# The first layer's output product: seven products over 1024 of its 1536 rows, or over all of them

## The chip, the core and the metric

The kernel runs on one NeuronCore of one Trainium2 chip. TensorE (PE) multiplies; VectorE (DVE) and ScalarE (ACT) do the elementwise work and empty PE's accumulators in PSUM; GpSimd (POOL) does small arithmetic and issues the transfers that add to their target on arrival; SyncE (SP) issues the other transfers. The metric is the device time of one execution in microseconds. An execution that was profiled has its own time and, inside it, the span of the trace.

## The reference

Two encoder layers over 512 tokens of width 1024. Layer 0 mixes by dilated window attention (8 heads, three dilations each), layer 1 by grouped attention; both also attend with 4 heads to 256 memory tokens. What matters here is the end of each layer, with its 1536 = 8 x 128 + 4 x 128 branch columns:

```python
    for i in range(DEPTH):
        h = rmsnorm(x, norm_g[i])
        mem_h = rmsnorm(mem, mem_norm_g[i])
        ...
        o_mem = memory_attention(q_mem, mem_h, w_mem_kv[i], mem_qn_g[i], mem_kn_g[i])
        y = jnp.concatenate([o_mix, o_mem], axis=-1) * jax.nn.silu(gate)
        x = x + jnp.einsum('bse,ed->bsd', y, w_out[i])
```

y is [512 tokens, 1536], w_out[i] is [1536, 1024]. In this document the 1536 rows of w_out[0] are named by the heads that feed them: the memory heads 8 to 11 (m), heads 0 to 3 (a) and heads 4 to 7 (b), 512 rows each.

## The kernel before

**Float32 in three passes.** Each weight tile of 128x1024 ("wl", half a megabyte) is loaded, cast by ACT to PE's rounded format ("wh", L324), and DVE takes the rest ("wo" = wl - wh, L334). The activations have a high and a low half too. A product is then high x high (L177), low x high (L178) and high x low (L181): L177 and L178 are issued together and need wh alone, L181 follows at the end of a group and needs wo.

**Seven products instead of eight.** `s_chunk` multiplies 2x2 block matrices with seven block products (12, 11, S1, S2, S4, S3, 22, in this order), from sums of weight tiles (T1 to T4) and of activation tiles (S1 to S4). Each product of 512x512 blocks is summed over the rows in groups. A **group** is 12 matmuls of 128x512 (or 24 of 128x256 for the gates and projections) that use up one weight tile; PE's work is a row of groups, and I call each a **slot**. The two halves of 128 tokens of a block go to two PSUM banks ("pj", four in all, handed out in turn; four more, "at", serve attention). A product marked True in `PRODUCTS` starts with cleared banks taken anew ("fresh"), one marked False adds to what its bank holds.

**The order is fixed when the program is built.** `Driver` steps a set of generators once a slot (`tick`); what they issue goes to the engines' queues in that order, and each engine works through its own queue strictly in order, waiting on semaphores. `drv.late` puts an instruction at the end of a slot's list, `drv.soon` at the beginning of the next one's, `drv.release(gen, d)` starts the emptying of a bank d slots on. `W` plans the weights by `PLAN`: loads on SP ("wl<-in_wall"), sums by DVE, or by transfers that POOL issues (L262, L298, L308), wh on ACT, wo on DVE, about two slots ahead of their use.

**The end of layer 0.** The eight heads and the three gates follow `A_ORDER`: heads 0 to 7, then the gates m, a, b. A gate (seven products of 128x256 matmuls) yields SiLU values (ACT L883, DVE L885), which are multiplied by the heads' outputs, reloaded from DRAM ("og", L861, L870; the product is DVE L875, L879). For m and a the results ("yf") are turned into the activations y12, y11, yS1, ... of the output product by `prep_y` (ACT L924 high half, DVE L925 low half; sums L940 to L955). Head 7's last part (`attn_a`: scales on ACT L1414, transposes on PE L1430, values on PE L1451) runs during the output product, with pauses from `Y`.

`out_proj` runs the output product in two pieces. Heads 8 to 11 and 0 to 3 (1024 rows) go through `s_chunk` in seven products of two groups, 14 slots. Each product's bank is copied by ACT to "acc" (L400) or added to it by DVE (L423), and the residual x is added to acc by a transfer (L1012). Then `out_rest` takes heads 4 to 7 (512 rows) as a plain product: 8 groups, each emptied by a DVE add into acc (L815). When both halves of a row block are done, `ev_o` stores x1, norms it (ACT squares L526, POOL L487, DVE L533) and transposes it into the inputs of layer 1 (PE L539). The memory keys and values of layer 1 (8 slots) are multiplied between this and the first product of layer 1, and cover that chain.

Counting slots from the start of the program, the gates take slots 141 to 161, the seven products 162 to 175, the plain product 178 to 185 (176 and 177 hold no PE work), the memory product 186 to 193, and layer 1 starts at 194. In the trace slot 162 starts at 561.1 us, slot 178 at 603.9, slot 186 at 627.4 and slot 194 at 652.8.

## Time and profile before

| what | value |
|---|---|
| median of three runs | 938.81 us (938.36 to 940.7) |
| profiled execution, its own time | 938.24 us |
| span of its trace | 936.5 us |
| busy in the span: PE, DVE, ACT, POOL | 928.6, 798.3, 691.4, 347.4 us |
| granted TensorE clock, mean | 1.000 |
| HBM read, written | 160.41 MB, 13.17 MB |

Most of the working below compares the profiled execution with itself, so 938.24 us is the scale of its sums; it lies 0.57 us under the median. In the profile's rows, "out<-in" names tiles, "x4" counts instructions, and a group's "idle before" tells what ended the engine's idle time. A matmul's listed duration is a latency; matmuls overlap, so what one costs is the distance between the starts of two. In the chain of waits, a piece is start, length, engine, tile, line.

### The profile page before, as it was taken

What the parts mean: (1) busy time and instruction counts of PE and PEld (TensorE: products, weight loads), DVE (VectorE), ACT (ScalarE), POOL (GpSimd) and SP (SyncE); (2) the same over time, 40 slices, a digit from 0 to 9 for tenths busy, and PEclk for the clock granted to TensorE, in tenths of its full rate; (3) what the DMA queues carried; (4) which work ended last, traced back from release to release, by engine and by line L of the source; (5) the groups of instructions that cost most, each with busy time, mean ns of one, the idle gap of its engine ahead of it and who ended that gap; (6) DMA issues with size and microseconds to landing.
All of it is one profiled execution on the core that took longest, in us unless ns stands there. A gap on an engine that the chain in (4) does not pass through costs nothing.

```text
span 936.5 us, 16241 instructions
## 1 busy us (share of the span) xinstructions
PE 928.6 (99%) x5468; PEld 816.2 (87%) x5468; DVE 798.3 (85%) x1442; ACT 691.4 (74%) x1720; POOL 347.4 (37%) x496
## 2 busy tenths in 40 slices
PE   8999999999999999999999999999999999999998
PEld 6889888888888888888889998888988999999886
DVE  6998677879888888879798999977998998789977
ACT  6775789677868686867675768547878887789774
POOL 3411425556554545463836111214162440111122
PEclk9999999999999999999999999999999999999999
DMA  9999948968687778686867989979995686785777
GB/s 345 387 266 332 296 129 211 322 150 241 166 243 174 237 162 266 158 270 135 269 154 210 249 232 218 300 245 313 273 199 114 175 243 166 197 215 131 197 164 180
DMA packets 83789, 209.25 MB, mean 223 GB/s; under 512 B 18937, under 2 KB 28665, under 8 KB 83706
## 3 DMA queue, kind: packets, MB, share of 16 engines
q1 hardware_dynamic: 63178, 142.74, 42.7%
q0 software_dynamic: 19520, 63.97, 37.0%
q10 hardware_dynamic: 1008, 1.51, 0.4%
q8 instruction: 43, 0.70, 0.3%
q14 instruction: 40, 0.33, 0.1%
HBM read 160.41 MB, written 13.17 MB: 185 GB/s over the span
## 4 chain that ended last, share of the span: by engine, by line
PE 95%; DVE 2%; ACT 1%; DMA 1%; issue 0%; SPq 0%; DVEq 0%; ACTq 0%
PE pj L177 25%; PE pj L178 25%; PE pj L181 25%; PE qT L654 3%; PE sa L1342 2%; PE oo L1451 2%; PE ptb L1657 1%; PE sa L1338 1%; PE xT L539 1%; PE pt L1430 1%; PE ob L181 1%; PE ob L178 1%; PE ob L177 1%; PE sb L172 1%; PE sb L171 1%; PE sb L173 1%
## 5 line engine op out<-in xcount | busy, mean ns | idle before, releaser
L334 DVE TENSOR_TENSOR wo<-wl,wh 128x1024 fp32r<-128x1024 f32 x258 | 316.4, 1232 | 7.0 <-ACT wh L324 6.8
L324 ACT CAST wh<-wl 128x1024 fp32r<-128x1024 f32 x258 | 271.9, 1060 | 31.3 <-PE pj L178 18.7
L177 PE MATMUL pj<-wh,hS 128*128 128x512 f32 (+1 forms) x416 | 154.4, 380 | 0.0
L178 PE MATMUL pj<-wh,hS 128*128 128x512 f32 (+1 forms) x416 | 149.0, 367 | 0.0
L177 PE MATMUL pj<-wh,h 128*128 128x512 f32 (+1 forms) x312 | 115.2, 378 | 0.0
L178 PE MATMUL pj<-wh,h 128*128 128x512 f32 (+1 forms) x312 | 111.6, 367 | 0.0
L487 POOL TENSOR_TENSOR rstd<-mse,half 128x4 f32<-128x4 f32 (+2 forms) x98 | 104.1, 1062 | 8.2
L181 PE MATMUL pj<-wo,hS 128*128 128x512 f32 (+1 forms) x416 | 99.5, 366 | 0.0
L178 PEld LDWEIGHTS pj<-wh,hS 128*128 128x128 f32 x416 | 78.7, 189 | 11.3
L177 PEld LDWEIGHTS pj<-wh,hS 128*128 128x128 f32 x416 | 78.6, 189 | 11.1 <-DVE sn L423 0.2
L486 POOL TENSOR_SCALAR mse<-hss 128x4 f32<-128x4 f32 (+1 forms) x88 | 47.1, 535 | 101.3 <-ACT junk L642 93.5
L181 PEld LDWEIGHTS pj<-wo,hS 128*128 128x128 f32 x416 | 72.5, 189 | 13.2
L642 ACT ACTIVATE junk<-sn 128x128 f32<-128x128 f32 x264 | 79.3, 310 | 2.2 <-DVE sn L413 2.1
L400 ACT COPY sn<-pj 128x512 f32<-128x512 f32 x122 | 67.3, 590 | 17.7 <-PE pj L181 17.7
L1285 POOL TENSOR_TENSOR ta<-sn,tabs 128x128 f32<-128x128 f32 (+1 forms) x64 | 35.8, 566 | 117.5 <-DVE sn L647 90.4
L181 PE MATMUL pj<-wo,h 128*128 128x512 f32 (+1 forms) x312 | 74.5, 365 | 0.0
L308 POOL DMA_DIRECT2D wl<-wl x34 | 30.2, 897 | 111.4 <-DVE wo L334 71.9
L262 POOL DMA_DIRECT2D wl<-in_wall_dram x40 | 38.0, 966 | 80.8 <-DMA wl<-in_wall_dram 32.2
L423 DVE TENSOR_TENSOR sn<-pj,sn 128x512 f32<-128x512 f32 x89 | 60.8, 684 | 6.9 <-PE pj L181 6.6
L178 PEld LDWEIGHTS pj<-wh,h 128*128 128x128 f32 x312 | 59.0, 189 | 8.3
L177 PEld LDWEIGHTS pj<-wh,h 128*128 128x128 f32 x312 | 59.0, 189 | 8.2
L181 PEld LDWEIGHTS pj<-wo,h 128*128 128x128 f32 x312 | 54.3, 189 | 9.7
(284 smaller groups left out, 2358.5 us busy)
## 6 DMA issues: line engine op xcount, KB each, us to landing
wl<-in_wall_dram SPq DMA_DIRECT2D x224, 512.0 KB, 9.2
wl<-wl POOLq DMA_DIRECT2D x68, 512.0 KB, 5.6
wl<-in_wall_dram POOLq DMA_DIRECT2D x44, 512.0 KB, 8.4
od<-o SPq DMA_DIRECT2D x11, 256.0 KB, 3.6
og<-od SPq DMA_DIRECT2D x10, 256.0 KB, 8.6
x<-in_x_dram SPq DMA_DIRECT2D x4, 512.0 KB, 9.1
v0r<-sn SPq DMA_DIRECT2D x8, 256.0 KB, 10.9
v0d<-v0r SPq DMA_DIRECT2D x4, 512.0 KB
```

Of the source, the lines that this page charges most:

```text
L177: T.matmul(o, a, b, start=start, stop=False, skip_group_check=True)
L178: T.matmul(o, c, d, start=False, stop=False, skip_group_check=True)
L181: T.matmul(o, a, b, start=False, stop=stop, skip_group_check=True)
L262: queue.dma_start(t, wall[d], **how)
L324: A.copy(wh, self.tile[self.items[i]])
L334: V.tensor_tensor(wo, self.tile[key], wh.bitcast(F32), ALU.subtract)
L400: A.copy(t_, b_)
L423: V.tensor_tensor(t_, b_, t_, ALU.subtract if q == "12" else ALU.add)
L486: G.tensor_scalar(e, ss, EPS, None, ALU.add)
L487: G.tensor_tensor(r, e, half[:, 0:n], ALU.pow)
L642: A.activation(jk, p[:, j * 128:(j + 1) * 128], AF.Square, scale=by, accum_out=ss[:, j:j + 1])
L1285: G.tensor_tensor(ta[:, 0:n], xn[:, 0:n, 0:32], ropeA[:, 0, b, s0:s0 + n], ALU.mult)
```

## The change

Heads 4 to 7's rows are no longer a separate plain product. A new weight kind, `W3`, loads 12 blocks of two tiles' width for **one** set of seven products over all 1536 rows: each product has three groups, two for the rows of m and a, and a third for the rows of b (heads 4 to 7), which takes its activations from a second set, `YL` (tiles "yl11", "ylS1" and so on), made by `prep_l`: high half by ACT L994, low half by DVE L997, sums by DVE (L1020 makes the one for ylS1). The products come in the order 11, S3, 12, S1, S2, S4, 22. `out_rest` and its additions go. The gates are computed in the order b, m, a. The evacuations are new: `hold` copies 11, S3 and S1's banks; `add_11` copies and adds by a transfer; `fold` sums by transfers and one DVE subtraction; x is added by transfers from `ahead` (for 22 and 21) and `ev_all` (for 11 and 12). T1's weight sums are made by a transfer from layer 0's last chunk on (`T1_DMA` 15). Head 7 takes its pauses from `Y_LAST`. `ev_o` is stepped when both halves are done, whichever is last.

```diff
-Y = [3, 2, 2, 2, 3, 2, 2, 1, 1, 1]
-
-A_ORDER = "01234567mab"
-
-PLAN = ["W2"] + ["T2"] * 2 + ["W1", "W2s"] + ["W2" if c.isdigit() else "W1" for c in A_ORDER[1:]] + ["W2"] + ["O1"] * 2 + ["T2b"] * 2 + ["W1bs", "W2c"] + ["W1b"] * 4 + ["W2b", "W1o"]
+Y, Y_LAST = [3, 2, 2, 2, 3, 2, 2, 1, 1, 1], [2, 2, 1, 1, 2, 1, 1, 1, 1, 1]
+
+A_ORDER = "01234567bma"
+
+PLAN = ["W2"] + ["T2"] * 2 + ["W1", "W2s"] + ["W2" if c.isdigit() else "W1" for c in A_ORDER[1:]] + ["W3"] + ["T2b"] * 2 + ["W1bs", "W2c"] + ["W1b"] * 4 + ["W2b", "W1o"]
 SEQ = [1, 2, 0] + list(range(3, len(PLAN)))
 T4_AT = {4: 4}
-T1_DMA = 17
+T1_DMA = 15
...
+    ORDER_3 = ("11", "T3", "21", "T1", "T2", "22", "T4")
+    LOADS_3 = (("11", "11"), ("T3", "12"), ("21", "21"), ("T1", "12"), ("T2", "22"), ("22", "22"))
...
-                    for k in ORDER:
+                    order, loads = ORDER, LOADS
+                    if kind == "W3":
+                        order, loads, n = ORDER_3, LOADS_3, 3
+                        for k in at:
+                            at[k].append(d + 8 + 2 * (k[1] == "2") + (k[0] == "2"))
+                    self.allocs += [((c, k, x), at[q][x], kind) for k, q in loads for x in range(n)]
+                    for k in order:
                         for x in range(n):
...
+    PRODUCTS_3 = (("11", 1, True), ("S3", 0, True), ("12", 0, True), ("S1", 0, True), ("S2", 1, False), ("S4", 0, False), ("22", 0, True))
+
...
+        def hold(name, u, b):
+            t = snap[name, u] = place({"z": "11", "s3": "21", "s5": "22"}[name], u)
+            A.copy(t, b)
+            yield 1
+            if name == "s5":
+                ahead("22", u, t)
+
+        def add_11(name, u, b):
+            t = s2(name="sn")
+            A.copy(t, b)
+            yield 1
+            G.dma_start(snap[name, u], t, accum_op=ALU.add)
+            yield 1
+            yield from ev("11", u, snap[name, u])
+
+        def fold(name, u, b):
+            t, t3, t5 = place("12", u), snap["s3", u], snap["s5", u]
+            snap[name, u] = t
+            A.copy(t, b)
+            yield 1
+            G.dma_start(t3, t, accum_op=ALU.add)
+            yield 2
+            V.tensor_tensor(t5, t5, t3, ALU.subtract)
+            ahead("21", u, t3)
+            yield 1
+            yield from ev("22", u, t5)
+
         after = ((keep, "z"), (add, "11", "z"), (keep, "s5"), (keep, "s2"), (add, "12", "s2"), (keep, "s3"), (add, "21", "s3"))
-        for i, (a, s, fresh) in enumerate(PRODUCTS[:6] + (("22", 1, False),) if tail else PRODUCTS):
+        order, runs = PRODUCTS[:6] + (("22", 1, False),) if tail else PRODUCTS, K // per
+        if late is not None:
+            order, runs = PRODUCTS_3, 3
+            after = (hold, "z"), (hold, "s3"), (add_11, "z"), (hold, "s5"), (fold, "s2"), (add, "12", "s2"), (add, "21", "s3")
+        for i, (a, s, fresh) in enumerate(order):
             while a not in act:
                 drv.tick()
             if fresh:
                 bank[s] = [pj() for _ in range(units)]
-            for x in range(K // per):
+            for x in range(runs):
+                far = late is not None and x == 2
+                while far and a not in late:
+                    drv.tick()
                 wh, wo = [...]
+                ah, al = [(late if far else act)[a][:, v] for v in range(2)]
...
+                        d = 2 if f in (keep, hold, fold) or late is not None or tight and i == 1 else 2 + u + (units == 1 and i == 6 and not soon)
...
-    def out_rest(ys, acc, done, evac):
...
+            if fused:
+                yield from wait((0, 0))
+                put("11", a11)
+                yield 1
+                yield from wait((0, 1))
+                s1 = [s2(name="ys") for _ in range(2)]
+                for j in range(2):
+                    V.tensor_tensor(s1[j], a11[j], a21[j], ALU.subtract)
+                yield 1
+                put("S3", s1)
+                yield 1
...
+                put("12", a12)
...
+                    V.tensor_tensor(a21[j], a21[j], a22[j], ALU.subtract)
+                yield 1
+                put("S1", a21)
...
+            if fused:
+                while ys[0] is None:
+                    yield 1
+                put("11", ys[0])
+                yield 1
+                while ys[1] is None:
+                    yield 1
+                s1 = s2(name="yl")
+                V.tensor_tensor(s1, ys[0], ys[1], ALU.subtract)
+                put("S3", s1)
+                yield 1
+                while ys[2] is None:
+                    yield 1
+                put("12", ys[2])
+                yield 1
+                while ys[3] is None:
+                    yield 1
+                a11, a21, a12, a22 = ys
+                V.tensor_tensor(a21, a21, a22, ALU.subtract)
+                put("S1", a21)
+                yield 2
+                V.tensor_tensor(a11, a21, a11, ALU.subtract)
+                put("S2", a11)
...
+        def ev_all(q, u, t):
+            b, n = 2 * (int(q[0]) - 1) + u, int(q[1]) - 1
+            if not b // 2:
+                G.dma_start(t, src[b][:, n * 512:(n + 1) * 512], accum_op=ALU.add)
+                yield 2
+            done.add((n, b))
+            if {(0, b), (1, b)} <= done:
+                yield from evac(n, b, acc[b])
+
+        def ahead(q, u, t):
+            b, n = 2 + u, int(q[1]) - 1
+            G.dma_start(t, src[b][:, n * 512:(n + 1) * 512], accum_op=ALU.add)
+
+        if not last:
+            s_chunk(512, YW, ev_all, half=half, tight=True, place=place, late=YL, ahead=ahead)
+            return
+        drv.spawn(prep_l())
         s_chunk(512, YW, ev, half=half, tight=True, place=place)
-        if not last:
-            out_rest(ys, acc, done, evac)
-            return
...
-        yield Y[7] + (h == 7)
+        yield Y[7]
...
-            if c == "b":
+            if c == A_ORDER[-1]:
                 drv.spawn(prep_y(), PREP_Y)
+                drv.spawn(ys[0](), PREP_Y)
...
-        if n:
-            for j in range(2):
-                nc.sync.dma_start(x1d[b][:, j * 512:(j + 1) * 512], x1[j])
-            r = norm_1(x1)
-            yield EO[0]
-            norm_2(x1, r, rows["x1"])
-            yield EO[1]
-            if b < 2:
-                first_t(H2, x1, b)
-            else:
-                yield from diffs_t(H2, x1, b - 2)
-                yield EO[2]
-                yield from rest_t(H2, b - 2, (EO[3] + b - 2, *EO[4:]), True)
+        for j in range(2):
+            nc.sync.dma_start(x1d[b][:, j * 512:(j + 1) * 512], x1[j])
+        r = norm_1(x1)
+        yield EO[0]
+        norm_2(x1, r, rows["x1"])
+        yield EO[1]
+        if b < 2:
+            first_t(H2, x1, b)
+        else:
+            yield from diffs_t(H2, x1, b - 2)
+            yield EO[2]
+            yield from rest_t(H2, b - 2, (EO[3] + b - 2, *EO[4:]), True)
```


In the changed program the seven products are slots 162 to 182 (21 groups, where 14 and 8 were), the memory product 183 to 190, and layer 1 starts at 191. It has 5294 matmuls on PE where it had 5306, 12 of 128x512 fewer. On the other engines: DVE 1442 instructions instead of 1444, with 11 adds from a bank into acc instead of 21 and 261 wo instead of 258; ACT 1310 instead of 1302, with 261 wh instead of 258; POOL 511 instead of 501; SP 367 instead of 365. Lines move down in the changed file: wh is L321, wo L331, a gate's SiLU L886 and L888, its product with the heads L878, y's halves L919 and L920, head 7's scales L1491 and its transposes L1507; the matmuls keep L177, L178 and L181.

**Order of ACT around the second and third product.** Before, ACT between the copies of the banks of S1 (pj_7237, pj_7238; 580.9 us in the trace) and those of S2 (pj_7177, pj_7178; 586.3 us):

```order
L400 COPY acc_7308<-pj_7237 128x512
L400 COPY acc_7309<-pj_7238 128x512
L324 CAST wh_7313<-wl_7023 128x1024
L924 CAST yS3_7318<-yf_6048 128x512
L924 CAST yS3_7318<-yf_6049 128x512
L324 CAST wh_7336<-wl_7129 128x1024
L165 CAST v0_7353<-v0_7141 128x512
L165 CAST pT_7341<-pt_7343 128x512
L165 CAST pT_7341<-pt_7348 128x512
L400 COPY acc_7191<-pj_7177 128x512
L400 COPY acc_7192<-pj_7178 128x512
```

Now, ACT from the copies of S3's bank (pj_7266, pj_7267) to those of 12's (pj_7334, pj_7335), in slots 168 to 171:

```order
L429 COPY acc_7348<-pj_7266 128x512
L429 COPY acc_7349<-pj_7267 128x512
L321 CAST wh_7354<-wl_7027 128x1024
L919 CAST yS1_7357<-yf_6435 128x512
L919 CAST yS1_7357<-yf_6436 128x512
L994 CAST yl12_7362<-sn_6325 128x512
L321 CAST wh_7378<-wl_7075 128x1024
L994 CAST ylS1_7387<-sn_6413 128x512
L321 CAST wh_7402<-wl_7119 128x1024
L919 CAST yS2_7408<-yf_6435 128x512
L919 CAST yS2_7408<-yf_6436 128x512
L436 COPY sn_7427<-pj_7334 128x512
```

Two casts for the third group (L994) now stand between the two pairs of copies, and the copies of 12's bank come behind the casts of yS2, three slots' worth of ACT's work behind the copies of S3's bank.

**Order of PE from 12 to S1.** Now, the end of the third group of product 12 and the start of S1, slots 170 and 171. Before, product 12 was the first, 11 (on another pair of banks) followed it, and S1 took 12's banks two groups later.

```order
L178 MATMUL pj_7335<-wh_7325,yl12_7362 128x512
L181 MATMUL pj_7334<-wo_7326,yl12_7362 128x512 x2
L181 MATMUL pj_7335<-wo_7326,yl12_7362 128x512 x2
L177 MATMUL pj_7413<-wh_7354,yS1_7357 128x512
L178 MATMUL pj_7413<-wh_7354,yS1_7357 128x512
```

S3 (pj_7266, pj_7267), 12 (pj_7334, pj_7335) and S1 (pj_7413, pj_7414) are all fresh and follow each other, while 11's banks (pj_7145, pj_7146) stay in use until S2 has been added to them; so these three products take the same two of the four banks, one after another.

**Order of head 7's transposes on PE.** Before, the second set of head 7's transposes stood behind the second group of S2, two groups behind the first set:

```order
L181 MATMUL pj_7177<-wo_7255,yS2_7164 128x512 x2
L181 MATMUL pj_7178<-wo_7255,yS2_7164 128x512 x2
L1430 MATMUL pt_7343<-ident_68,p_6627 128x128 x4
L1430 MATMUL pt_7348<-ident_68,p_6627 128x128 x4
L177 MATMUL pj_7237<-wh_7276,yS4_7257 128x512
```

Now it stands behind the first group of product 11 (slot 162), one group behind the first set (pt_7135):

```order
L1507 MATMUL pt_7135<-ident_68,p_6535 128x128 x4
L177 MATMUL pj_7145<-wh_7024,y11_6884 128x512
...
L181 MATMUL pj_7145<-wo_7025,y11_6884 128x512 x2
L181 MATMUL pj_7146<-wo_7025,y11_6884 128x512 x2
L1507 MATMUL pt_7170<-ident_68,p_6534 128x128 x4
L1507 MATMUL pt_7175<-ident_68,p_6534 128x128 x4
```

The tile p_6534 that they read is written by the last of ACT's scales (L1491). The transposes moved from the fourth product to the first, and closer together.

More of the change, by code (lines that the diff above doesn't have):

```diff
@@ L206, in __init__ @@
                     units, nb = GROUPS[kind]
-                    if kind == "O1":
-                        n = PLAN[c - 1] == "O1"
-                        for x in range(2):
-                            self.items.append((c, "P", x))
-                            self.last.append(g + 5)
-                            self.allocs.append(((c, "P", x), d + x, kind))
-                            self.users[c, "P", x] = 1
-                        self.need += [base + 2] * 2 if not n else [base + 2] * 6
-                        g += 2 if not n else 6
-                        units = 0
                     for u in range(units):
@@ L416, in add @@
             t = snap[name, u]
-            if name == "s3":
+            if name == "s3" and late is None:
                 diff(u)
@@ L462, in s_chunk @@
                             drv.half()
-                    st = fresh and kk == 0 and (units == 2 or b == 0)
+                    st = fresh and x == k == 0 and (units == 2 or b == 0)
                     if tokens:
@@ L890, in ev @@
                         yield 1
+                        asked.clear()
                         load()
-                    if not all(h in o_here for h in hs):
+                    if asked:
                         yield 1
@@ L899, in ev @@
                 yield 1
[L900 to L909 removed]
+                ys[2 * j + i] = t
             s_chunk(256, H, ev, tokens=False, half=half, soon=g == 2, turn=turn)
```

105 lines of the change are left out of this document (46 added, 59 removed).

## The prediction

> **What bounds the kernel now.** I read the page first: the busy row of the engines, the granted clock, the chain that ended last, and then PE's waits.
>
> ```profile
> PE 928.6 (99%) x5468; PEld 816.2 (87%) x5468; DVE 798.3 (85%) x1442; ACT 691.4 (74%) x1720; POOL 347.4 (37%) x496
> PEclk9999999999999999999999999999999999999999
> PE 95%; DVE 2%; ACT 1%; DMA 1%; issue 0%; SPq 0%; DVEq 0%; ACTq 0%
> PE row L1145 <- DMA row<-in_mem_norm_g_dram: 2.3, 1, 2.3
> PE pmt L781 <- DVE pmT L787: 0.7, 1, 0.7
> ```
>
> PE carries 95% of the chain, its two longest recorded waits come to 3.0 us in 936.5, and 2.3 of these are at the very start. Busy time alone would prove little, because a listed matmul duration is a latency. So I looked in the chain of waits at what a group costs. Here are the L181 quarters of four groups in succession, the last of the seven products and the first three of the plain product that the change removes:
>
> ```profile
> 603.12 0.91 PE pj L181 x4
> 605.84 0.91 PE pj L181 x4
> 608.56 0.91 PE pj L181 x4
> 611.28 0.91 PE pj L181 x4
> 612.19 0.87 PE xT L539 x8
> ```
>
> Each starts 2.72 us after the last: a group of 12 matmuls costs 2.72 us, 0.227 each, with nothing between (608.56 to 611.28). The step from 603.12 to 605.84 crosses the two slots without PE work (176, 177), which therefore cost nothing. PE issues at a steady rate here, so the end moves by what is taken from PE and by what PE is newly made to wait, and by nothing else.
>
> **The change, part by part.**
>
> *Matmuls.* 14 + 8 groups become 21; one group of 12 goes: **-2.72 us**. This is the whole possible gain, 0.29% of 938.8. About 0.3%, 2.8 us, is what a measurement of this kernel can tell from no change, so the full gain stands just at that line.
>
> The Trainium skill's page "TensorE: Matmul & The Clock Gate", section "Back-to-back issue gap", gives N/2.4 + 2.5 ns for a warm matmul, 216 ns at 512 columns. By that a group would be 2.59 us and the gain 2.59. The trace's 227 ns is the measured thing, and the sum uses it.
>
> *Head 7's transposes, now one group apart.* The rows of ACT and DVE before:
>
> ```profile
> 573.69 0.17 DVE L1403 TENSOR_SCALAR c<-c 128x8 f32<-128x8 f32 x1
> 573.90 1.71 ACT L1414 ACTIVATE p<-p,c 128x256 f32<-128x256 f32 x4 [0.53 <-DVE c L1403]
> 577.62 0.44 PE pt L1430 x4
> 578.97 1.60 ACT L1414 ACTIVATE p<-p,c 128x192 f32<-128x192 f32 x4
> 583.56 0.88 PE pt L1430 x8
> 654.82 0.96 PE pj L181 x8
> ```
>
> Before, the second scales ended at 580.57 and their transposes came at 583.56, 3 us to spare. Now ACT must do, from c on: 4 scales (1.71), a copy (0.53), a cast wh (0.95), two casts (1.04), a SiLU of the same size (0.52) and 4 scales (1.60), 6.4 us with the spacings quoted below. PE reaches the second transposes after its group 161 (24 matmuls at 0.96/8 = 0.12, 2.9), 4 transposes (0.44) and group 162 (2.72), 6.0 us, if c is ready as PE starts slot 161. **+0.4 us**; nothing if DVE's c comes 0.4 earlier, 1.3 if it comes 0.9 later. Behind the scales in ACT's queue stands the cast of the next wh; it has over a slot of slack.
>
> *Banks of S3, 12 and S1.* Three fresh products now share two banks. The first matmul of 12 has to wait until ACT has copied S3's bank. The trace has no such wait; its parts are in the last product before 598.6:
>
> ```profile
> 597.68 0.91 PE pj L181 x4
> 598.17 1.07 ACT L400 COPY acc<-pj 128x512 f32<-128x512 f32 x2 [2.07 <-PE pj L181]
> L400 ACT COPY sn<-pj 128x512 f32<-128x512 f32 x22 | 12.6, 592 | 7.9 <-PE pj L181 7.9
> ```
>
> The L181 quarter ends its first bank with its second matmul, which starts at 597.91; the waiting copy starts at 598.17 and takes 0.59. PE would hear of it some 0.05 later (as at 13.38 to 13.43, rows further down), at 598.81; the next group starts at 598.59. So **+0.25 us**. The second bank's copy ends behind 12's first four matmuls (0.91) and adds nothing. ACT is free at that point: ahead of these copies stand wh casts that need nothing late. Bounds 0.1 and 0.8.
>
> From 12 to S1 ACT isn't idle. What stands ahead of the copies of 12's banks is in the order shown above: yS1, yl12, wh, **ylS1**, wh, yS2 twice. ylS1 needs DVE's sum L1020, and DVE does ahead of it the low half of yl12 (L997), and two sums (L947). The spacings, from rows that stand close together:
>
> ```profile
> 582.84 1.14 ACT L924 CAST yS<-yf 128x512 fp32r<-128x512 f32 x2
> 583.88 1.05 ACT L324 CAST wh<-wl 128x1024 fp32r<-128x1024 f32 x1
> 584.83 0.63 ACT L165 CAST v<-v 128x512 fp32r<-128x512 f32 x1
> 579.05 1.29 DVE L925 TENSOR_TENSOR yS<-yf,yS 128x512 fp32r<-128x512 f32 x2
> 580.25 1.22 DVE L334 TENSOR_TENSOR wo<-wl,wh 128x1024 fp32r<-128x1024 f32 x1
> 581.39 1.29 DVE L955 TENSOR_TENSOR yf<-yf 128x512 f32<-128x512 f32 x2
> 560.00:580.00 20.00, 20.00 (x97) 16.73 (x96) 19.72 (x35) 15.36 (x28) 4.35 (x5) 1.00 0.94 223
> ```
>
> ACT: 1.04 for two casts, 0.95 for wh. DVE: 1.20 for two tensor operations (0.6 each), 1.14 for wo. DVE is busy 19.72 of 20 us up to 580, so in this stretch it runs its list through and lags behind PE. I laid the rows of both engines one behind the other from slot 158 on with these spacings. Let T be the start of slot 170 on PE, the third group of 12. DVE ends yl12's low half at T - 0.35; then L947 twice, T + 0.9; L1020, T + 1.5. ACT then casts ylS1 (0.52, T + 2.05), wh (T + 3.0), yS2 (T + 4.05), and the first copy ends at T + 4.65; PE starts S1 at T + 4.7. Dense it would start at T + 2.72: **+2.0 us**. If DVE is 1 us ahead of my list, 1.0; if the copies stand free, 0.25 as above; if DVE is 1.4 behind, 3.4. S2 takes no fresh bank, and S1's three groups (8.2 us) give ACT and DVE time to catch up: no stall behind it.
>
> *yl12 for slot 170.* Its high half is ready early; its low half, done at T - 0.35, is needed by L178, the second matmul of the group (T + 0.23): a slack of 0.6. **+0.1**, at most 0.8 if DVE is 1.4 behind.
>
> *Transfers.* The sums T1 of W3 move from DVE to POOL's queue; x's additions move from L1012 to L1089 and L1081.
>
> ```profile
> wl<-wl POOLq DMA_DIRECT2D x68, 512.0 KB, 5.6
> wl<-in_wall_dram POOLq DMA_DIRECT2D x44, 512.0 KB, 8.4
> og<-od SPq DMA_DIRECT2D x10, 256.0 KB, 8.6
> acc<-in_x_dram POOLq DMA_DIRECT2D x8, 256.0 KB, 6.9
> DMA to landing us min/median/max: 2.0/5.4/8.9
> L1012 POOL DMA_DIRECT2D acc<-in_x_dram x8: 862/878/1161, 577.8 to 606.8; - x8
> ```
>
> The weights are issued at least two slots (5.4 us) beyond their landing time ahead of wh; nothing. POOL's queue issues one accumulate in 0.88 us. The last ones decide: behind DVE's L449 in slot 181 two transfers from `ahead` (0.88 each, 6.9 to landing), then two adds from 22's bank (1.28), then DVE's wo for slot 185: 0.88 + 6.9 + 1.28 + 1.14 = 10.2 us. Everything on DVE behind these adds waits with them, and PE waits for that wo. PE has slots 181 to 184, two of 2.72, two of 3.6 with transposes, plus 1.8 until the L181 of slot 185, 14.4 us, of which L449 is late by some 2.9 us: slack 1.3. At a landing of 8.9 (the longest of the tile acc) it would be a stall of 0.7. The norm behind it has a slack of about 1 us up to slot 188. **+0.2**, bounds 0 and 3.
>
> *Gate order and shorter pauses.* The gates' groups are the same; DVE and ACT do the same there, and PE's trace has no wait in the stretch up to 561 us: 0, bounds -0.2 and +0.5.
>
> Sum: -2.72 + 0.4 + 0.25 + 2.0 + 0.1 + 0.2 = **+0.2 us**. Against the profiled execution, 938.24, that is 938.5; against the median of 938.81, which is 0.57 above it, 939.0. I take **939.0**: the change gives back what it saves.
>
> **The rivals.**
>
> *The stalls are hidden.* If DVE stands 1.5 us better than my list, ACT copies 12's bank as it is done, and the waits are 0.25 twice and 0.3 besides: -2.72 + 0.8 = -1.9; with all hidden, -2.7. For: DVE has 11 adds into acc instead of 21, and the head's tail is behind it earlier. Against: most of the adds saved come later than slot 170, and DVE was busy 19.72 of 20 us. Time 936.1 to 936.9.
>
> *A late transfer stops DVE's queue (slower).* In slots 164 to 167 DVE multiplies with og's, which must land between their issue and the use about two slots on; and in 183 it adds to acc. If a landing is 8.9 and its issue held back by a full ring, DVE stops and ACT's copies behind L994 with it, first at slot 171. For: the wait DVE has for og in this trace is 0.4 us, so the loads land not long ahead. Against: the last og was issued at 562.7 and used at 576.1, 13.4 us later, against 8.6 to landing. It decides from about 2 us beyond the median landing; then 2 us at 171 and 1 to 2 us at 185 to 188 come on top: 942.5 to 944.
>
> ```profile
> L875 DVE TENSOR_TENSOR yf<-sn,og 128x512 f32<-128x512 f32 x8 | 5.5, 684 | 0.4 <-DMA og<-od 0.4
> L861 SPq DMA_DIRECT2D og<-od x10: 377/418/2181, 497.0 to 562.7; - x10
> L875 DVE TENSOR_TENSOR sn<-sn,og x2: 680/683/686, 559.9 to 576.1; 128x512 f32<-128x512 f32 x2
> ```
>
> *PE's clock falls in the stall at S1 (slower).* At the start of the program PE runs at half rate after it has been idle:
>
> ```profile
> 8.74 0.43 PE pj L177
> ...
> 12.06 0.60 ACT act L165
> 12.68 0.70 DVE act L168
> 13.43 0.50 PE pj L178
> 13.92 0.23 PE pj L177
> ```
>
> 0.43 us a matmul in the beginning, 0.23 from 13.9 on, and the pause of 1.4 us while ACT and DVE made an operand (12.06 to 13.43) did not slow what came behind it. If the stall at slot 171 is long enough, some 10 matmuls cost 0.2 more each, 2 us. With a stall of 3.4 instead of 2.0: 939.0 + 1.4 + 2 = 942.4.
>
> The same page of the Trainium skill, section "HAM oscillation — how this bites in real kernels", has it that an idle gap of more than about 3.4 us puts the clock back to half. The first slow matmuls here agree with a cold start; no gap of 3.4 us within this trace shows the fall.
>
> **How the numbers follow.** The forecast, stalls of 1.5 to 4.5 us in all that eat the 2.72, 0.52 (own range 937.5 to 940.7). Stalls mostly hidden 0.29. Late transfers 0.13. Clock 0.06. Range 936.2 to 942.6: it leaves out the upper half of the two slower cases and a little of the full gain. Faster by over 0.3% (below 936.0) needs the whole 2.72 and something more: 0.08. Slower by over 0.3% (above 941.6): the late transfers, most of the clock case and a tail of the forecast, 0.19. Within 0.3%: 0.73.
>
> **What would show it.** Right: PE's waits list a wait for ACT's copies (L436 for S1's first matmul, about 2 us; L429 for 12's, about 0.25), and a wait of the transposes L1507 for ACT L1491; seven products of 21 groups in about 57.1 us dense plus attention; layer 1 starts some 2.9 us later than 21 dense groups would give. Wrong: no wait of PE on L436 above 0.6 (then the first rival), or DVE waiting for og or acc above 1 us (the second), or matmuls of 0.43 behind slot 171 (the third). Were PE slowed in the gates, from 509 to 561 us, my zero for the new order would fall.

## The result, and the profile after the change

The changed kernel takes **960.2 us** (959.78 to 961.67) against 938.81: a ratio of 1.0233, 95% interval 1.0222 to 1.0244. It is 21.4 us slower, where 939.0 with a range up to 942.6 was predicted. The profiled execution took 960.2 us, its span is 958.4. The page of after, its rows for the engines, the granted clock and the chain:

```profile
PE 935.0 (98%) x5456; PEld 817.6 (85%) x5456; DVE 799.3 (83%) x1440; ACT 696.7 (73%) x1728; POOL 360.9 (38%) x506
PEclk9999999999999999999999998997999999999999
PE 27%; DVE 5%; DMA 4%; ACT 3%; issue 2%; POOL 1%; DVEq 0%; POOLq 0%; ACTq 0%
```

The 12 matmuls are gone (5468 to 5456). The chain that ended last reaches back only to 563.1 us here, so its shares make 42% and not 99%; of these 42 PE has 27, where before it had nearly all. The clock row has a dip in slices 25 to 28 (575 to 671 us): what was lost lies there. PE's waits of after:

```profile
PE xT L572 <- ACT f L633: 4.6, 2, 3.4
PE pj L181 <- DVE wo L331: 4.4, 3, 2.6
PE pj L177 <- ACT yl L994: 2.5, 1, 2.5
PE pj L178 <- DVE yl L997: 2.1, 1, 2.1
PE pj L177 <- ACT sn L436: 0.7, 1, 0.7
PE pj L177 <- ACT acc L429: 0.2, 1, 0.2
```

From the starts of PE's stages in the two timelines:

| stage | before | after | difference |
|---|---|---|---|
| up to the output product | 561.11 | 561.55 | +0.4 |
| output product, until the memory product | 66.30 | 73.59 | +7.3 (dense: -2.7) |
| memory product, until layer 1 | 25.34 | 38.55 | +13.2 |
| layer 1, until the last matmul ends | 279.55 | 280.65 | +1.1 |

So 10.0 us were lost in the product and 13.2 behind it. In both a late transfer takes part.

**In the product: two loads of og that took 15 and 16.6 us.** SP's timeline of after (the issues), then DVE's, with the idle time before an instruction in brackets:

```profile
565.47 0.38 SPq L863 DMA_DIRECT2D og<-od  x1
570.21 0.38 SPq L863 DMA_DIRECT2D og<-od  x1
```

```profile
574.77 1.21 DVE L331 TENSOR_TENSOR wo<-wl,wh 128x1024 fp32r<-128x1024 f32 x1
580.48 0.69 DVE L878 TENSOR_TENSOR yf<-sn,og 128x512 f32<-128x512 f32 x1 [4.50 <-DMA og<-od]
586.86 0.69 DVE L878 TENSOR_TENSOR yf<-sn,og 128x512 f32<-128x512 f32 x1 [3.95 <-DMA og<-od]
```

DVE stands still for 8.4 us in front of the two products, and everything behind them in its queue with it: the wo's, yl12's low half, the sums. The transfers between 560 and 590 us show why. Before, then after (each row: target and source, queue, count, KB, median us to landing):

```profile
DMA packets 3025, 6.81 MB, mean 227 GB/s; under 512 B 455, under 2 KB 1416, under 8 KB 3022
wl<-in_wall_dram SPq DMA_DIRECT2D x9, 512.0 KB, 9.6
```

```profile
DMA packets 3050, 8.52 MB, mean 284 GB/s; under 512 B 289, under 2 KB 1201, under 8 KB 3048
wl<-in_wall_dram SPq DMA_DIRECT2D x7, 512.0 KB, 14.6
```

A quarter more bytes pass in a window of 30 us, and a weight lands after 14.6 us instead of 9.6 (medians). Of the 24 half-megabyte transfers that `W3` needs from DRAM (18 loads, 3 sums T1, 3 sums T3), 18 were there before. The stretches show it as DMA share (the column before the last), the clock before it; first before, then after:

```profile
575.00:590.00 15.00, 15.00 (x82) 12.79 (x81) 15.00 (x21) 15.00 (x28) 1.84 (x3) 1.00 0.82 198
```

```profile
575.00:590.00 15.00, 13.35 (x57) 10.05 (x55) 6.55 (x11) 5.60 (x8) 3.51 (x4) 1.00 1.05 289
590.00:600.00 10.00, 5.06 (x12) 3.34 (x12) 9.58 (x15) 5.54 (x9) 0.86 (x1) 0.66 0.95 190
```

Before, DVE was the busy one here (15.00 of 15) and the transfers had room, though not in the 15 us ahead of it, where their share was 0.99 (after: 1.01). After, DVE works 6.55 of 15 us and the transfer engines are full. What PE loses is best read from the starts of its groups, since a stall's price has the slowed clock in it:

```profile
585.40 0.39 PE L177 MATMUL pj<-wh,y 128*128 128x512 f32 x1
...
588.74 1.20 PE L181 MATMUL pj<-wo,y 128*128 128x512 f32 x4 [1.36 <-DVE wo L331]
592.45 0.80 PE L177 MATMUL pj<-wh,yl 128*128 128x512 f32 x1 [2.52 <-ACT yl L994]
595.36 0.80 PE L178 MATMUL pj<-wh,yl 128*128 128x512 f32 x1 [2.11 <-DVE yl L997]
...
596.38 0.63 PE L178 MATMUL pj<-wh,yl 128*128 128x512 f32 x1
596.81 0.63 PE L177 MATMUL pj<-wh,yl 128*128 128x512 f32 x1
...
600.28 0.50 PE L177 MATMUL pj<-wh,yS 128*128 128x512 f32 x1 [0.66 <-ACT sn L436]
```

Two groups of 2.72 take 7.05 (585.40 to 592.45) and 7.83 us (to 600.28): 4.3 + 5.1 = 9.4 of the 10.0. Matmuls at 0.43 instead of 0.227 are among them. How much of this is og's is a question for a run in which og is on time.

**Behind the product: transfers in series, with DVE's list between them.** The chain of waits of after, from `fold`'s transfer on (start, length, engine, tile), then two rows of POOL and one of DVE:

```profile
617.58 8.31 DMA acc<-acc
625.94 7.96 issue
...
635.06 9.92 DMA acc<-in_x_dram
645.00 0.73 ACT sq L559 x2
```

```profile
633.91 1.77 POOL L1089 DMA_DIRECT2D acc<-in_x_dram  x2 [14.57 <-DVE acc L449]
635.06 2.41 POOL L1081 DMA_DIRECT2D acc<-in_x_dram  x2
642.44 0.69 DVE L422 TENSOR_TENSOR acc<-pj,acc 128x512 f32<-128x512 f32 x1 [4.82 <-DMA acc<-in_x_dram]
```

`fold`'s transfer takes 8.3 us. Only when it has landed can DVE subtract (L449), and only then may x be added to the tile of 21 (L1089). DVE's subtraction itself comes only at 632.87, 7 us after the first landing; ahead of it in DVE's list stand two operations (L422) that had waited for the same transfers. POOL stands 14.57 us in front of L1089 for it, and the transfers behind L1089 in POOL's queue stand with it: x for 12 (L1081), whose landing of 9.9 us is the one in the chain. DVE waits 4.82 us for L1089's landing before its next add (L422), and the wo's come behind that. So the squares of the norm start at 645.0; the norm's chain from there to the transposes ends at 662.2, and PE has stood idle in front of them for 3.4 us by then. PE's groups there: 4.1 + 1.0 lost between 640.99 and 651.45 (wo behind the adds, 2.65 + 0.40, and slow matmuls), 3.6 ahead of the transposes at 662.23, 2.3 within them and 2.0 in the slow group behind: 13.0 of the 13.2.

### The profile page after: what moved, and what is told of

Read it like the earlier page. It is cut to its first block, busy times and chain, and to the rows that moved or that the text cites. A ratio compares the mean times of both kernels' runs of the same rounds, so it can differ in the third digit from the quotient of the medians.

```text
span 958.4 us, 16243 instructions
## 1 busy us (share of the span) xinstructions
PE 935.0 (98%) x5456; PEld 817.6 (85%) x5456; DVE 799.3 (83%) x1440; ACT 696.7 (73%) x1728; POOL 360.9 (38%) x506
## 5 line engine op out<-in xcount | busy, mean ns | idle before, releaser
L331 DVE TENSOR_TENSOR wo<-wl,wh 128x1024 fp32r<-128x1024 f32 x261 | 319.6, 1229 | 10.2 <-ACT wh L321 9.9
L321 ACT CAST wh<-wl 128x1024 fp32r<-128x1024 f32 x261 | 275.3, 1060 | 27.0 <-PE pj L178 16.5
L177 PE MATMUL pj<-wh,hS 128*128 128x512 f32 (+1 forms) x416 | 154.4, 380 | 0.0
L178 PE MATMUL pj<-wh,hS 128*128 128x512 f32 (+1 forms) x416 | 149.1, 367 | 0.4 <-DVE hS L651 0.4
L177 PE MATMUL pj<-wh,h 128*128 128x512 f32 (+1 forms) x312 | 115.2, 378 | 0.0
L178 PE MATMUL pj<-wh,h 128*128 128x512 f32 (+1 forms) x312 | 111.6, 367 | 0.0
L520 POOL TENSOR_TENSOR rstd<-mse,half 128x4 f32<-128x4 f32 (+2 forms) x98 | 101.8, 1039 | 8.2
L181 PE MATMUL pj<-wo,hS 128*128 128x512 f32 (+1 forms) x416 | 99.5, 366 | 0.0
L178 PEld LDWEIGHTS pj<-wh,hS 128*128 128x128 f32 x416 | 78.7, 189 | 11.9 <-DVE hS L651 0.6
L177 PEld LDWEIGHTS pj<-wh,hS 128*128 128x128 f32 x416 | 78.6, 189 | 10.9
L181 PEld LDWEIGHTS pj<-wo,hS 128*128 128x128 f32 x416 | 72.5, 189 | 13.1
L1360 POOL TENSOR_TENSOR ta<-sn,tabs 128x128 f32<-128x128 f32 (+1 forms) x64 | 38.3, 606 | 108.5 <-DVE sn L680 84.9
L259 POOL DMA_DIRECT2D wl<-in_wall_dram x44 | 41.8, 999 | 94.5 <-PE pt L1507 25.2
L181 PE MATMUL pj<-wo,h 128*128 128x512 f32 (+1 forms) x312 | 74.5, 365 | 0.0
L305 POOL DMA_DIRECT2D wl<-wl x35 | 31.4, 905 | 102.1 <-DVE wo L331 60.6
L422 DVE TENSOR_TENSOR sn<-pj,sn 128x512 f32<-128x512 f32 x89 | 60.8, 684 | 6.9 <-PE pj L181 6.6
L178 PEld LDWEIGHTS pj<-wh,h 128*128 128x128 f32 x312 | 59.0, 189 | 8.3
L177 PEld LDWEIGHTS pj<-wh,h 128*128 128x128 f32 x312 | 59.0, 189 | 8.2
L295 POOL DMA_DIRECT2D wl<-wl x35 | 32.9, 974 | 87.6 <-DMA wl<-in_wall_dram 16.1
```

The source lines that it names most:

```text
L177: T.matmul(o, a, b, start=start, stop=False, skip_group_check=True)
L178: T.matmul(o, c, d, start=False, stop=False, skip_group_check=True)
L181: T.matmul(o, a, b, start=False, stop=stop, skip_group_check=True)
L259: queue.dma_start(t, wall[d], **how)
L321: A.copy(wh, self.tile[self.items[i]])
L331: V.tensor_tensor(wo, self.tile[key], wh.bitcast(F32), ALU.subtract)
```

## The experiments

All of them compute the whole result; each ratio is against the kernel before on the same chip.

**Is it the bytes?** One line of after: layer 0's last sums T1 by DVE again, three transfers of half a megabyte less.

```diff
-T1_DMA = 15
+T1_DMA = 16
```

> The changed kernel, with the three T1 weight sums of W3 made by a DVE add again instead of a transfer that adds in flight (three transfers of 512 KB less). Theory (bytes): in the changed kernel the transfer engines are full from before 560 to 590 us, and the last two og loads take 14.9 and 16.6 us behind the weights; 3 x 0.52 MB at about 285 GB/s are 5.5 us of that. So og lands about 5 us earlier, the loss of 9.3 us up to the first group of S1 falls to 2 to 4 us, and the loss of about 13 us in slots 185 to 191 stays: about 954 us. Rival (place): og is late because of where it is issued, behind weights whose number is the same on SP's queue; then the three transfers on POOL's queue do not matter and the time stays within 1.5 us of 960.

Measured: 952.97 us, ratio 1.0138 (1.0100 to 1.0176), 7.2 faster than after. The transfers from 560 to 590 us, and PE's waits:

```profile
og<-od SPq DMA_DIRECT2D x3, 256.0 KB, 5.5
```

```profile
PE xT L572 <- ACT f L633: 4.3, 2, 3.5
PE pj L178 <- DVE yl L997: 2.2, 1, 2.2
PE pj L177 <- ACT sn L436: 2.1, 1, 2.1
```

The last og lands after 5.5 us, and DVE waits for none of them, though SP issues the last one later than in after, at 574.27. The product takes 70.27 us instead of 73.59: only 3.3 of its 10.0 us come back, and in exchange DVE has three sums more to do. With og on time a stall of the size predicted at S1 is there, 2.1 us, and as long a one for yl12's low half. I had expected the stage behind to keep its length; it fell from 38.55 to 32.93. The number of transfers isn't shown to be the cause of that: two kernels below that keep every transfer (old_pauses, old_gates) have 32.65 and 32.77 there too. All three are without the 5.1 us at the wo's, and the first x for 21 lands in 6.6, 4.3 and 4.8 us in them instead of 8.4. Why it lands sooner I can't say.

**Is the rest `fold`'s transfer?** DVE adds instead:

```diff
-            G.dma_start(t3, t, accum_op=ALU.add)
-            yield 2
+            V.tensor_tensor(t3, t3, t, ALU.add)
```

> The changed kernel, with the sum of S3's and S2's banks in `fold` made by a DVE add of the copied tile instead of a transfer (L447), and without its pause of two slots. Theory (tail by itself): the loss of about 13 us in slots 185 to 191 starts with L447 (8.3 us to land), after which L449, x's transfer L1089 (9.9 us) and DVE's adds follow; without it L1089 is issued about 10 us earlier, DVE's wait in slots 183 to 185 goes (3 us of PE's waits and the slow clock behind them), and what is left is x's transfer for product 12 (L1081, about the 4.6 us of waits at L572): about 953 us, with the first loss of 9.3 us unchanged. Rival: the tail is late only because everything before it is late by 9 us; then it stays at 960.

Measured: 950.7 us, 1.0114 (1.0064 to 1.0163), 9.5 faster. The memory product's stage takes 26.39 us instead of 38.55, the product 73.95 as in after. So the path through `fold`'s transfer was the cause of the tail, and it wasn't late merely because the work ahead of it was. The edit takes out the transfer and the two slots of pause behind it together; no run parts the two. PE's wait for the transposes, 4.6 in after, is

```profile
PE xT L571 <- ACT f L632: 0.7, 1, 0.7
```

**Both, and x for 12 by a load.** The two edits together; besides, x of 12's blocks is loaded in `hold` to a tile of its own and subtracted by DVE in `fold`, so that 12 needs no transfer that adds at the end (`ev_all` then adds x for 11 alone, not shown):

```diff
+                x12[u] = s2(name="xr")
+                nc.sync.dma_start(x12[u], ahead("12", u, None))
...
             ahead("21", u, t3)
+            V.tensor_tensor(t, t, x12[u], ALU.subtract)
```

> Both edits, and x for the product 12 no longer added by a transfer at the end (L1081) but loaded to a tile of its own while S1 runs and subtracted by DVE from the copy in `fold` (the final result is bank minus that tile). If bytes and the two late transfers are all: the first loss 2 to 4 us, the tail 0 to 2 us: 939 to 943 us. If the gate order or the pauses have a cost of their own that the two losses only hid: 945 or more.

Measured: 943.33 us, 1.0044 (1.0031 to 1.0056), 16.9 less than after, just beyond what was expected. 7.2 and 9.5 make 16.7, but that they add so well is luck. By stages the two gains overlap behind the product (5.6 and 12.2 apart, 13.3 together: the memory product takes 25.29 us, as before the change), they make 3.65 in the product (69.94), layer 1 gives 1.2 back (281.85), and there is a third edit. What is left is on PE in the product:

```profile
590.47 0.50 PE L178 MATMUL pj<-wh,yl 128*128 128x512 f32 x1 [1.90 <-DVE yl L1001]
595.40 0.50 PE L177 MATMUL pj<-wh,yS 128*128 128x512 f32 x1 [2.13 <-ACT sn L440]
595.97 0.62 PE L177 MATMUL pj<-wh,yS 128*128 128x512 f32 x1
596.39 0.63 PE L178 MATMUL pj<-wh,yS 128*128 128x512 f32 x1
```

yl12's low half 1.9, S1's bank 2.13, and behind them 8 matmuls at 0.43.

**The pauses and the gate order, each undone in after.** First the pauses:

```diff
-    YS = Y, Y_LAST
+    YS = Y, Y
...
-        yield Y[7]
+        yield Y[7] + (h == 7)
```

> The changed kernel with head 7's pauses as they were (Y for all heads, and one slot more before its second transposes). Theory: the pauses only move head 7's small work; og and the tail stay late: within 2 us of 960. Rival: the earlier tail of head 7 crowds DVE and ACT in slots 161 to 165 and so delays the gate's products and the release of og's buffers: 955 or less.

Measured: 963.97 us, 1.0255 (1.0217 to 1.0293): 3.8 slower than after, so the shorter pauses are worth 3.8 here; neither of the two expectations holds. By stages it is 9.7 more in the product (83.29) and 5.9 less behind it. PE's wait for yl12's high half is 4.8 instead of 2.5, and it newly waits 3.5 for head 7's probabilities:

```profile
PE oo L171 <- ACT pT L165: 2.2, 1, 2.2
PE oo L172 <- DVE pT L168: 1.3, 1, 1.3
```

Then the order of the gates:

```diff
-A_ORDER = "01234567bma"
+A_ORDER = "01234567mab"
```

> The changed kernel with the gates in the old order m, a, b, and nothing else undone. The third group's activations (heads 4 to 7) then come from the last gate, and the third group of product 11 (slot 164) needs them. Theory: og of the last gate is as late as in the changed kernel, and the first group that needs it is slot 164 and not 170: PE waits some 10 us more, 965 to 972 us. Rival: the new gate order is what makes og late, and with the old one the loss shrinks: 955 or less.

Measured: 955.52 us, 1.0176 (1.0145 to 1.0206): 4.7 **faster** than after. In the old order the last og is issued at 565.56 and multiplied at 579.85 without a wait:

```profile
565.56 0.45 SPq L863 DMA_DIRECT2D og<-od  x1
579.85 0.69 DVE L878 TENSOR_TENSOR sn<-sn,og 128x512 f32<-128x512 f32 x1
```

So the new gate order, which I had put at nothing, is part of what makes og late: its last load goes out at 570.21. But that isn't where the gain lies. The product takes 72.94 us, 0.65 less than in after, since PE then waits for other operands (2.3 for yl11's low half, 2.7 for the two of ylS); the rest is the stage behind, 32.77 instead of 38.55.

**Is it T1's transfer as such?** The kernel before with the one line of the change:

```diff
-T1_DMA = 17
+T1_DMA = 15
```

> The kernel before, with the two T1 sums of its seven-product output weights made by a transfer that adds in flight instead of by DVE (two transfers of 512 KB more, two DVE adds less). Theory: there the last og load has 13.4 us between issue and use against 8.6 to land; 1.05 MB at about 285 GB/s are 3.7 us more, which still fits: within 1 us of 938.8. Rival: that stage of the kernel before is at the edge of the transfer engines too, and og becomes late there: 941 or more.

Measured: 938.52 us, 0.9997 (0.9986 to 1.0007). Nothing. Two such sums by transfer cost nothing in a kernel that had a DMA share of 0.99 from 560 to 575 us and of 0.82 from 575 to 590; three cost 7.2 us in after.

**Can the product's own stalls go?** From here on each kernel stands on the one before it. First, in t1_fold_x12, the copies of the banks are issued without the two slots of delay, and the products of the gate hand their operands over a slot earlier:

```diff
-                        drv.release(f(*arg, u, bank[s][u]), d)
+                        gen = f(*arg, u, bank[s][u])
+                        if f in (hold, add_11):
+                            drv.urgent.append([drv.slot + 1 + next(gen), gen])
+                        else:
+                            drv.release(gen, d)
...
                 times(t)
-                yield 1
                 ys[2 * j + i] = t
```

> The kernel of t1_fold_x12 (T1 by DVE, the sum in `fold` by DVE, x for product 12 by DVE), with two moves in the order: the copies of the banks of 11, S3, S1 and 12 are issued right behind the product's last group, ahead of the next slot's casts, and the third group's activations of heads 4 to 7 are handed on one slot earlier, so that yl12's low half stands on DVE ahead of yS1's. Theory (queues in order): in t1_fold_x12 PE still waits 1.9 us for yl12's low half and 2.1 us for the copies of 12's banks, which stand behind ylS1, wh and yS2 on ACT, and then runs 8 matmuls at about half rate (2 us). With the copies first the second wait is 0.25, the first is near 0, and the slow clock is gone: 943.3 - 1.9 - 1.9 - 2.0 = 937.5 us, 1.3 below the kernel before. Rival: DVE itself is too late, by the three T1 sums that it makes, and the order on ACT does not matter: 942 to 943.5.

Measured: 942.44 us, 1.0035 (1.0023 to 1.0048). yl12's wait fell from 1.9 to 0.45, but S1's stayed. ACT, and PE's first matmul of S1:

```profile
590.43 0.62 ACT L1001 CAST ylS<-sn 128x512 fp32r<-128x512 f32 x1 [2.81 <-DVE sn L1027]
590.95 1.99 ACT L321 CAST wh<-wl 128x1024 fp32r<-128x1024 f32 x2
592.85 1.06 ACT L440 COPY sn<-pj 128x512 f32<-128x512 f32 x2
```

```profile
593.48 0.50 PE L177 MATMUL pj<-wh,yS 128*128 128x512 f32 x1 [2.05 <-ACT sn L440]
```

ACT stands 2.81 us in front of the cast of ylS1, for DVE's sum, and two wh's come ahead of the copies. That is the stall of the prediction in its place, its way through ylS1 and its size, with two wh's where the working had one and two casts of yS2. With T1 by transfer in this better order (T1_DMA 15):

> The same, but with the three T1 sums of W3 by transfers that add in flight, as in the changed kernel. Theory (bytes): the transfer engines are full again up to 590 us, og lands 15 us after its issue, DVE waits for it by about 8 us and PE by 5 to 9 us behind it: 943 to 947 us. Rival: with the copies and activations in better order there is room enough, and DVE has 3.4 us less to do: 937 or less.

Measured: 945.78 us, 1.0072 (1.0048 to 1.0095): three transfers still cost 3.3 (two runs, 944.52 and 947.05), and DVE waits 6.7 us for og again.

Next, ylS1's preparation is moved behind the copies:

```diff
                 V.tensor_tensor(a21, a21, a22, ALU.subtract)
-                put("S1", a21)
                 yield 2
+                put("S1", a21)
+                yield 1
```

> copies_first, with the cast of ylS1 (third group of S1, used in slot 173) issued two slots later, so that on ACT nothing that waits for DVE stands ahead of the copies of 12's banks. Theory (ACT's queue, and the clock behind a stall): in copies_first PE waits 2.05 us for these copies, and then 11 of the following matmuls start 0.43 us apart instead of 0.23, about 2 us more. Without the wait both go: 942.4 - 1.8 - 2.0 = 938.6 us; what is left against the dense count is 1.3 us at slot 195 (an input of layer 1). Rival: the slow matmuls have another cause than the wait; then 940.6.

Measured: 941.64 us, 1.0029 (1.0018 to 1.0040). S1's wait is down to 0.22, but a new one of 1.8 stands at the transposes of the memory rows:

```profile
620.88 1.71 PE L580 MATMUL xT<-ident,m 128*128 128x128 f32 x8 [1.84 <-issue]
```

DVE shows what is late, its subtraction in `fold`, which waits for x:

```profile
615.07 0.69 DVE L452 TENSOR_TENSOR acc<-acc 128x512 f32<-128x512 f32 x1 [2.75 <-DMA acc<-in_x_dram]
```

On top of this a shorter pause in the norm (EO 2, 2, 1, 1, 2, 1). It is aimed at another wait, the 1.3 us for ACT's L732 at layer 1's start:

> The same, with one pause of `ev_o` shorter by a slot (between the inputs S2 and S4 of layer 1). Theory: PE's wait of 1.3 us at the fourth product of layer 1 is for the high half of S4's input, which ACT and DVE make one slot too late because layer 1 now begins three slots earlier; with it one slot earlier the wait is gone: 937.3 us, below the kernel before by 1.5 (0.16%). Rival: that wait is for the engines' time and not for the pause: the same as the run without this edit.

Measured: 942.03 us, 1.0033 (1.0020 to 1.0045): no gain. The wait for L732 is gone, but a matmul now waits 2.1 us for DVE's L422 instead; 1.25 us of the stall at the transposes stay.

For that stall, in yls1_later, x for 22 is added after the subtraction, not ahead of it:

```diff
             if name == "s5":
-                ahead("22", u, t)
...
             V.tensor_tensor(t5, t5, t3, ALU.subtract)
+            ahead("22", u, t5)
             ahead("21", u, t3)
```

> yls1_later, with x for product 22 added behind DVE's subtraction in `fold` instead of ahead of it, so that the subtraction no longer waits for that transfer. Theory: in yls1_later the two subtractions wait 2.9 us in all for x's transfers (8.5 us to land, the transfer engines are full up to 620 us), DVE then normalises the memory rows late, PE waits 1.8 us for them at 620.9 and 5 matmuls behind it run at half rate (1 us). Without it: 941.6 - 2.8 = 938.8 us. What is left is 1.3 us at 666 us and 0.8 us at the banks: equal to the kernel before. Rival: the memory rows are late for another reason (their own loads): 941 or more.

Measured: 939.68 us, 1.0008 (1.0000 to 1.0017), 20.5 less than after, and the stall at the transposes is gone. Its profiled execution took 939.25, span 937.5. What PE still waits for in the product, and at layer 1's start:

```profile
PE pj L177 <- ACT kmT L732: 1.3, 1, 1.3
PE pj L178 <- DVE yl L1004: 0.6, 1, 0.6
PE pj L177 <- ACT acc L431: 0.2, 1, 0.2
PE pj L177 <- ACT sn L439: 0.2, 1, 0.2
```

The product takes 65.15 us, 1.15 less than before the change; the memory product 25.29, the same; layer 1 gives 2.26 back. 1.34 of that is one wait at 662.26 for ACT's L732; before the change PE did not wait there, and in after, whose stalls come ahead of it, it doesn't either. The other 0.9 I did not trace. One more shortening of the norm's pauses (EO 2, 1, 1, 2, 2, 1) on top:

> The same, and the pause between the norm of x1 and its transposes one slot shorter, so that the inputs of layer 1 are made 2.7 us earlier. Theory: the 1.3 us at 666 us are DVE's lag with these inputs (PE's wait there ends with DVE's copy of a bank behind them), and go: 937.5 to 938 us. Rival: PE then waits for the norm at the transposes instead: the same as x22_later or slower.

Measured: 940.84 us, 1.0019 (1.0010 to 1.0028), no gain: PE then waits 0.8 at the transposes and 1.7 for an operand of layer 1 (ACT L658). No version beat the kernel before.

## Why the prediction was wrong, step by step

- **The first step that failed: "The weights of W3 are issued at least two slots (5.4 us) beyond their landing time ahead of wh; nothing."** The landing time was taken from before's trace, with 18 transfers in a stretch that had a DMA share of 0.99 and 0.82. Six more filled it, and landing went from 9.6 to 14.6 us for weights. Worse, og suffered, which shares the queue and has the shorter slack: DVE stood 8.4 us for it. Three transfers less alone give 7.2 us back (t1_on_dve), 3.3 of them in the product.
- **The rival of the late transfer was the right mechanism with the wrong price.** It had DVE stop at og and again at acc, and these are the two places. But its "against" (13.4 us between og's issue and use, 8.6 to landing) compared a slack of before with a landing of before. In after DVE came to the products 10.5 and 12.7 us after og's issue (565.47 to 575.98, 570.21 to 582.9), and the landing took 15.0 and 16.6. I had put 2 us on PE at this place. The two groups behind the wait lost 9.4, but the product still loses 6.7 of its 10.0 when og is on time and DVE makes the T1 sums instead, so og's own part, between 3.3 and 9.4, isn't shown more closely. The chance of 0.13 rested on that comparison.
- **The second, and larger: x's transfers in the tail, +0.2 with bounds 0 and 3; the stage lost 13.2 us.** The working followed one transfer (6.9 us to landing) to one wo. The path has two in series, `fold`'s 8.3 and x's 9.9, with 8.0 us between them in which DVE's list comes to the subtraction. `fold`'s was listed in the change and never followed to its end. fold_on_dve takes 12.2 us out of that stage; 5.6 to 5.9 of them also go in three kernels that keep `fold`'s transfer.
- **Gate order, 0 with bounds -0.2 and +0.5: 4.7 in after.** PE's trace shows nothing in the gates, as predicted (561.11 and 561.55). The cost lies behind: the order sets when the last og is issued, and undoing it takes 0.65 us out of the product and 5.8 out of the stage behind in the profiled run. The pauses were put at nothing with it; undone, they cost 3.8 in after.
- **S1's bank, +2.0: the way is right, the size in part luck.** 0.66 in after, where everything ahead of it had stalled already; 2.1 in t1_on_dve and 2.05 in copies_first, through ylS1 and the wh's ahead of the copies. But there DVE also makes the three T1 sums, which my list did not have; in copies_first one of them (579.01) stands in DVE's list without a gap up to ylS1's sum at 589.71. old_gates, with the sums by transfer and no wait for og, has 0.2 at this bank. No run has the forecast's order with og on time. What was missing is the clock behind the stall (below), 8 matmuls at 0.2 more, 1.6 us.
- **12's bank, +0.25: 0.22.** yl12's low half, +0.1 with at most 0.8: 1.9 in t1_fold_x12, 0.45 with the operands a slot earlier; DVE was further behind than my list, again with the T1 sums on it. Head 7's transposes, +0.4: no wait in after.
- **One group less, -2.72: right**, as far as it can be seen: in x22_later the product has waits of 0.23 + 0.63 + 0.22 = 1.1 and is 1.15 shorter, 0.5 short of the sum.
- **The clock rival** had its chance with a stall of 3.4 us. In copies_first it came with one of 2.05, in other runs not with stalls as long (below): its chance was underrated, not its price.

Without the two failed steps the forecast would still have been short: t1_fold_x12, which takes both out, measured 943.3, 4.3 more than 939.0 and just outside the range. After the fact, 939.0 plus 1.8 more at yl12, 1.6 of clock and 1.3 at the wait in layer 1, less the 0.6 of head 7's transposes and x's transfers that did not show, makes 943.1.

## What to carry to other kernels

A landing time belongs to the traffic it was measured in: when a change adds transfers to a stretch, first add up its bytes, and where the DMA share is already near 1 ahead of a load, don't trust the old landing, least of all for the load with the shortest slack. Follow each new transfer to the next thing that touches the same tile, and to what stands behind that in the same queue; two in series cost both landings. Give the terms that are put at nothing the same working as the large ones: here the weights, the gate order and x's transfers, 0.2 us in the sum together, made up most of the result.

## What the runs showed of the hardware

- **Landing under load.** The last og load, 256 KB, took 5.5 us with 259 GB/s over the stretch (t1_on_dve); two such loads took 15.0 and 16.6 us, by the end of DVE's waits, with 284 GB/s (after). The DMA share at the time doesn't tell them apart: it was 1.03 during the 5.5 us too. The time ahead differs: 0.72 from 570 to 574.3 us in t1_on_dve, 0.94 or more from 560 us on in after.
- **PE's clock can fall after a stall of about 2 us, and need not.** In copies_first one stall of 2.05 us (593.48), with no longer one near it, is followed by matmuls 0.43 us apart from 595.36 on, 1.9 us after it ended, for some 3 us:

```profile
595.36 0.63 PE L178 MATMUL pj<-wh,yS 128*128 128x512 f32 x1
```

  In yls1_later a single stall of 1.84 us is followed by matmuls 0.43 apart at once (622.81 to 624.52). But three stalls that were longer are followed by none, at a granted clock of 1.00: 2.12 us in yls1_later_eo (664.90), 2.29 in old_gates (572.47) and this one in old_pauses, with the matmuls from 584.54 on 0.23 apart:

```profile
583.51 1.19 PE L181 MATMUL pj<-wo,y 128*128 128x512 f32 x4 [2.25 <-DVE wo L331]
```

  A stall of 1.34 (x22_later, 662.26) was followed by none either. So its length alone doesn't decide, and what else does stays open. The Trainium skill's page "TensorE: Matmul & The Clock Gate", section "HAM oscillation — how this bites in real kernels", sets the fall at an idle gap of more than about 3.4 us. The falls behind 1.84 and 2.05 us disagree with it, and the measurement decides here. After's window 590 to 600 us has a granted clock of 0.66.
- **A smooth kernel shows waits that stalls had hidden.** The wait of 1.3 us for ACT's L732 at layer 1's start is in x22_later and copies_first, not in after.
